# Output projection of a hybrid decoder layer: column groups 2 and 3 as seven products of quarters

## The chip, the core and the metric

The kernel runs on one core of a Trainium2 chip. Its time is the device time of one execution in microseconds (us). An execution is one launch; nothing is computed on the host but a rearrangement of the weights.

## What is computed

One layer on 512 tokens of width 2048, in float32. Two token mixers (latent attention with 16 heads, and a gated spatial unit) give `merged`; then come one output projection, a gate from the conditioning vector, a residual and a final norm. The change touches the last three lines:

```python
c_act = jax.nn.silu(c)                               # c: one row of 2048
mod = c_act @ w_ada + b_ada                          # w_ada: 2048 x 6144
shift, scale, gate = jnp.split(mod, 3, axis=-1)
...
merged = jax.nn.sigmoid(g_mla) * y_mla + jax.nn.sigmoid(g_sgu) * y_sgu   # 512 x 2048
x = x + gate[:, None] * (merged @ w_out)             # w_out: 2048 x 2048
return rmsnorm(x, final_norm_g)
```

## The kernel before, in words

**Products.** TensorE multiplies float32r operands. Each operand is held as a high part (rounded, `hi`) and a low part (the rest, `lo`), and one product takes three matmuls: hi·hi, lo·hi and hi·lo (`mm3`, L156). Weights arrive as raw float32 tiles of 128x1024 (`wraw0` to `wraw2`, 512 KB each). The class `Stream` keeps a list of them in the order of use: it loads up to three ahead on the DMA queue of SP, and splits a tile when it is asked for: ACT rounds it to `w0h` or `w1h` (L121), DVE subtracts to `w0l` or `w1l` (L122).

**The projection.** `merged` stands transposed, one tile of 128 channels x 512 tokens for each of 16 heads: `mh[j]`, `ml[j]` (tile names `b` and `g`). The output has four groups of 512 columns (`cg`) and four blocks of 128 tokens (`n`). `out_granule(cg, i, ...)` (L1784) takes one weight tile, which holds two heads of one column group, and issues 2 x 4 x 3 = 24 matmuls of 128x512 into four PSUM banks: 16 with the high weights (L1795, L1796), then 8 with the low ones (L1793). Eight granules make a group. Granules (0,0) to (0,4) lie beside the last heads of the attention. The last stage, which the change rewrites, has the granules (0,5) to (0,7), groups 1 and 2, and then group 3 in another order: token block by token block, all 16 heads with `mm3`, so that a block ends when its 48 matmuls have run; the last block is done in two halves of 256 columns.

**What stands beside it.** The gate of columns 1024 to 2047 isn't ready yet: eight chunks `wada` of 128x2048 are loaded, multiplied by `cact` and summed on DVE (`chunk_sum`, L1943). `gbc` holds the gate, `gfb` the final gain, both broadcast to all partitions; `yt` holds x and then y for the whole output. `residual` (L1986) takes a finished bank: DVE multiplies by the gate and adds x, ACT squares with a sum (`ssy`), POOL multiplies by the gain. When a token block is complete, `ry` becomes 1/rms (DVE reduce and scale, ACT square root at L2028, DVE reciprocal at L2029), DVE and ACT scale y, and SP issues four DMAs of 256 KB to `out`.

**What sets the order.** Every engine and every DMA queue runs its instructions in the order in which the program writes them; a wait of one holds back all behind it. Nothing reorders them.

**Names that come with the change.** The seven-product scheme cuts an output of 2x2 quarters and an inner dimension of two halves; it needs 7 products instead of 8, and sums of quarters as operands. The kernel uses it earlier already, for the input projections, with a list `V7` of 28 passes (7 products x 4 weight tiles).

Of the kernel before, what the change touches and what calls it, by code (L numbers as in the profile page):

```python
# [20 lines left out]
P = 128  # L21
# [116 lines left out]
def trunk_layer(ctx, tc, xT, xn, c, vecs, pos, wada, w1, w2, wv, wv3, wv4, wh, wh15, wq, wqr, wk, wvv, wo, wsT, bsp, gfin, out,  # L138
# [102 lines left out]
    p_d = [scratch(f"p_d{i}", [10, P, P]) for i in range(2)]  # L241
    latn_d = [scratch(f"latn_d{i}", [P, S]) for i in range(10)]
# [76 lines left out]
    dp = [None]  # L319
    dlast = []  # L320

    def last_tiles():
        k = len(dlast)
        p = last_of[k // 4].p
        dlast.append((nt(p, [P, GW], F32R, f"dh{k}"), nt(p, [P, GW], F32R, f"dl{k}")))
        return dlast[-1]

    last_of = [None, None]
    for cg in range(3):
        for i in range(cg == 0, 8):  # L330
            go[cg, i] = ws.add(wo[cg, i], GW)
            if cg == 2 and i < 6:
                go[3, i] = ws.add(wo[3, i], GW, to=last_tiles)
    for i in (6, 7):
        go[3, i] = ws.add(wo[3, i], GW)
# [1415 lines left out]
    def merge_a(h, ps, turned_, gate_):  # L1751
# [173 lines left out]
    dp[0] = Scope("out", side=RIGHT)  # L1925
    grow = nt(dp[0].p, [P, D], F32, "gbc")
    gfb = nt(dp[0].p, [P, D], F32, "gfb")
    yt = nt(dp[0].p, [P, NB, D], F32, "y")
    last_of[0] = Scope("last", side=RIGHT)
    da = Scope("ada2")  # L1930
    cact = nt(da.p, [P, D], F32, "cact")
    DMA.dma_start(cact, bcast(cact_d, D))
    chunks, later = {}, {}

    def grow_load(cg):
        cols = slice(cg * S, (cg + 1) * S)
        DMA.dma_start(grow[:, cols], bass.AP(tensor=gate_row.tensor, offset=gate_row.offset + cg * S, ap=[[0, P], [1, S]]))

    def chunk_load(j):
        chunks[j] = nt(da.p, [P, D], F32, "wada", bufs=2)  # L1940
        DMA.dma_start(chunks[j], wada[2 * KC + j])

    def chunk_sum(j):  # L1943
        t = chunks.pop(j)
        stt(t, t, 1.0, cact, ALU.mult, ALU.mult, accum_out=dots[:, 2 * KC + j:2 * KC + j + 1])
        if j % 4 == 3:
            gate_sum(j - 3, j + 1)


    for j in range(NG, NG + 2):  # L1950
        chunk_load(j)
    chunk_at = dict(zip(range(NG, KC), (4, 5, 7, 8, 10, 11, 13, 14)))
    for j, st in chunk_at.items():
        later.setdefault(st, []).append(lambda j=j: chunk_sum(j))
        if j + 2 < KC:
            later[st].append(lambda j=j: chunk_load(j + 2))
    rows = []
    for cg, k in ((2, 1), (3, 4)):
        st = chunk_at[4 * cg + 3] + 1
        later.setdefault(st, []).append(lambda cg=cg, k=k: rows.append(  # L1960
            gate_turn(4 * cg, 4 * cg + 4, bank_at(k), nt(tp, [P, S], F32, "sig", bufs=3))))
        later.setdefault(st + 1, []).append(lambda: rows.pop()())
        later.setdefault(st + 2, []).append(lambda cg=cg: grow_load(cg))

    def no_more_chunks():
        da.close()
        last_of[1] = Scope("last1", side=RIGHT)

    later[chunk_at[KC - 1]].append(no_more_chunks)
    def gain_part(q):  # L1970
        cols = slice(q * S, (q + 1) * S)
        DMA.dma_start(gfb[:, cols], bass.AP(tensor=gfin.tensor, offset=gfin.offset + q * S, ap=[[0, P], [1, S]]))

    for cg in range(NG // 4):
        grow_load(cg)
# [33 lines left out]
    while pend:  # L2009
        pend.pop(0)()  # L2010
# [102 lines left out]
```

## Time and profile before

| what | value |
|---|---|
| median of 3 runs | 1530.39 us (1530.23 to 1530.84) |
| the profiled execution, its own time | 1528.86 us |
| its span in the profile | 1527.1 us |
| granted TensorE clock | 0.999 of full speed |
| matmuls | 7104 |
| last stage, first matmul to last | 1370.69 to 1519.62 us of the span |

The span runs from the first instruction to the last; launch and finish are the 1.8 us beside it. In a row of the timeline the first number is the start in us from the span's start, the second the duration, and what stands in brackets is the idle time ahead of it with what ended it. SPq is SP's DMA queue: its rows are the issues of transfers. A TensorE row's duration is longer than its distance from the next, since matmuls are pipelined; the distance is what counts.

### The profile page before, as it was taken

The page shows a single profiled execution, that of the slowest core. Times are in us where ns is not written, and L with a number is a line of the kernel's source. Part 1 is how long each engine was busy: PE and PEld are TensorE (multiplying, and loading weights), DVE is VectorE, ACT ScalarE, POOL GpSimd, SP SyncE. Part 2 cuts the span into 40 slices and gives each one's busy share as a digit, 9 for nine tenths or more (in the row PEclk, how much of TensorE's full clock was granted, in tenths as well). Part 3 has the DMA queues.
Part 4 walks back from the last instruction along what each step waited for, and adds up shares of the span by engine and source line. Part 5 has one row for each costly group of instructions (what it writes and reads, how often), then busy time and mean ns, then how long its engine had stood idle before and what let it go on. Part 6 is the DMA issues. An engine that isn't in the chain of part 4 may idle for free.

```text
span 1527.1 us, 20628 instructions
## 1 busy us (share of the span) xinstructions
PE 1515.8 (99%) x7104; PEld 1268.9 (83%) x7104; DVE 1219.4 (80%) x1656; ACT 816.2 (53%) x1280; POOL 241.2 (16%) x268
## 2 busy tenths in 40 slices
PE   9999999999999999999999999999999999999998
PEld 7888888888888888888888888888888888888887
DVE  8989897768787889888889797878788989856653
ACT  4444665546555556545555556556776677632331
POOL 0000000101010120311040203030242223321120
PEclk9999999999999999999999999999999999999999
DMA  9979876858887796868686967787788888769723
GB/s 376 388 273 349 246 201 171 236 144 239 249 224 188 203 242 198 227 205 215 199 212 188 226 200 188 230 210 215 191 211 204 212 197 231 180 169 348 247 99 111
DMA packets 336427, 337.68 MB, mean 221 GB/s; under 512 B 105801, under 2 KB 279937, under 8 KB 331201
## 3 DMA queue, kind: packets, MB, share of 16 engines
q1 hardware_dynamic: 310082, 306.46, 64.7%
q0 software_dynamic: 26240, 29.89, 11.5%
q8 instruction: 56, 0.92, 0.2%
q14 instruction: 49, 0.40, 0.1%
HBM read 302.12 MB, written 34.17 MB: 220 GB/s over the span
## 4 chain that ended last, share of the span: by engine, by line
PE 91%; DVE 3%; DMA 2%; SPq 1%; ACT 1%; issue 1%; POOL 1%; DVEq 0%; ACTq 0%
PE ps L1476 18%; PE ps L1477 18%; PE ps L1474 18%; PE ps L468 5%; PE ps L1795 3%; PE ps L1796 3%; PE ps L1793 3%; PE ps L158 2%; PE ps L159 2%; PE ps L157 2%; PE ps L477 2%; PE ps L478 2%; PE ps L480 2%; PE ps L1577 2%; PE ps L1578 2%; PE ps L1580 2%
## 5 line engine op out<-in xcount | busy, mean ns | idle before, releaser
L145 DVE TENSOR_TENSOR X<-X,X 128x1024 fp32r<-128x1024 f32 (+2 forms) x111 | 130.5, 1182 | 28.5 <-ACT X L699 27.1
L699 ACT CAST X<-X 128x1024 fp32r<-128x1024 f32 x70 | 73.7, 1053 | 95.7 <-PE ps L1477 55.7
L699 ACT CAST w0h<-X 128x1024 fp32r<-128x1024 f32 x70 | 73.7, 1052 | 93.2 <-PE ps L1477 50.5
L699 ACT CAST w1h<-X 128x1024 fp32r<-128x1024 f32 x69 | 72.6, 1052 | 76.2 <-PE ps L1477 37.1
L145 DVE TENSOR_TENSOR w0l<-X,w0h 128x1024 fp32r<-128x1024 f32 x70 | 85.5, 1221 | 28.8 <-ACT w0h L699 28.7
L145 DVE TENSOR_TENSOR w1l<-X,w1h 128x1024 fp32r<-128x1024 f32 x69 | 84.2, 1221 | 23.5 <-ACT w1h L699 23.5
L145 DVE TENSOR_TENSOR X<-wraw,X 128x1024 f32<-128x1024 f32 (+1 forms) x65 | 79.4, 1221 | 17.8 <-ACT X L699 16.9
L664 POOL DMA_DIRECT2D X<-in_wh x9 | 11.6, 1292 | 509.9 <-DVE w1l L145 166.6
L1477 PE MATMUL ps<-w1h,hl 128*128 128x512 f32 x236 | 91.8, 389 | 0.0
L1476 PE MATMUL ps<-w1h,hh 128*128 128x512 f32 x236 | 91.8, 389 | 0.0
L1476 PE MATMUL ps<-w0h,hh 128*128 128x512 f32 x236 | 91.8, 389 | 0.0
L1477 PE MATMUL ps<-w0h,hl 128*128 128x512 f32 x236 | 91.8, 389 | 0.0
L121 ACT CAST w0h<-wraw 128x1024 fp32r<-128x1024 f32 (+3 forms) x61 | 52.7, 864 | 71.9 <-PE ps L1796 22.9
L1476 PE MATMUL ps<-X,hh 128*128 128x512 f32 x232 | 90.4, 390 | 0.0
L1477 PE MATMUL ps<-X,hl 128*128 128x512 f32 x232 | 90.3, 389 | 0.0
L148 DVE SCALAR_TENSOR_TENSOR wada<-wada,cact 128x2048 f32<-128x2048 f32 x39 | 88.9, 2281 | 0.4 <-DMA wada<-in_wada 0.4
L122 DVE TENSOR_TENSOR w0l<-wraw,w0h 128x1024 fp32r<-128x1024 f32 (+3 forms) x61 | 61.7, 1012 | 34.4 <-ACT w0h L121 20.7
L121 ACT CAST w1h<-wraw 128x1024 fp32r<-128x1024 f32 (+3 forms) x60 | 52.5, 875 | 55.4 <-issue 13.2
L145 DVE TENSOR_TENSOR wraw<-wraw,X 128x1024 f32<-128x1024 f32 x66 | 80.4, 1218 | 0.9 <-DMA X<-in_wv 0.5
L122 DVE TENSOR_TENSOR w1l<-wraw,w1h 128x1024 fp32r<-128x1024 f32 (+3 forms) x60 | 62.7, 1045 | 20.0 <-ACT w1h L121 10.4
L1736 POOL TENSOR_TENSOR d<-turned,d 128x384 fp32r<-128x384 f32 (+1 forms) x48 | 42.7, 918 | 191.8 <-ACT d L1735 191.8
L1474 PE MATMUL ps<-w0l,hh 128*128 128x512 f32 x236 | 63.1, 389 | 0.0
(469 smaller groups left out, 4463.1 us busy)
## 6 DMA issues: line engine op xcount, KB each, us to landing
X<-in_wh SPq DMA_DIRECT2D x131, 512.0 KB, 5.0
wada<-in_wada SPq DMA_DIRECT2D x39, 1024.0 KB, 8.7
wraw<-in_wo SPq DMA_DIRECT2D x32, 512.0 KB, 4.5
wraw<-in_wh SPq DMA_DIRECT2D x21, 512.0 KB, 6.5
wraw<-in_wh POOLq DMA_DIRECT2D x21, 512.0 KB, 7.1
turned<-p_d SPq DMA_DIRECT2D x64, 160.0 KB, 4.6
X<-in_wv SPq DMA_DIRECT2D x17, 512.0 KB, 4.5
X<-in_wh SPq DMA_DIRECT2D x22, 384.0 KB, 4.9
```

Of the source, the lines that this page charges most:

```text
L121: self.nc.scalar.copy(hi[:, :n], raw[:, :n])
L122: self.nc.vector.tensor_tensor(out=lo[:, :n], in0=raw[:, :n], in1=hi[:, :n].bitcast(F32), op=ALU.subtract)
L145: DVE.tensor_tensor(out=out, in0=in0, in1=in1, op=op)
L148: DVE.scalar_tensor_tensor(out=out, in0=in0, scalar=scalar, in1=in1, op0=op0, op1=op1, **kw)
L468: PE.matmul(ps1[m], a[:, cols[m]], b, start=(j == 0 and a is wH and b is hh[j]), stop=False)
L699: ACT.copy(hi, t)
L1474: PE.matmul(to, xh[:, tk], wL[:, k], start=False, stop=sp, skip_group_check=True)
L1476: PE.matmul(to, xh[:, tk], wH[:, k], start=st, stop=False, skip_group_check=True)
L1477: PE.matmul(to, xl[:, tk], wH[:, k], start=False, stop=False, skip_group_check=True)
L1793: PE.matmul(banks[n], mh[j][:, tk], wL[:, sl], start=False, stop=j == H - 1)
L1795: PE.matmul(banks[n], mh[j][:, tk], wH[:, sl], start=j == 0, stop=False)
L1796: PE.matmul(banks[n], ml[j][:, tk], wH[:, sl], start=False, stop=False)
```

## The change

The granules (0,5) to (1,7) stay (eleven "wide" granules). Groups 2 and 3 become one block of 28 "tall" passes of 12 matmuls of 128x512. Its products are called 1 to 7; the list `E7` gives their order, two products interleaved at first (1 with 6, 2 with 7), then 3, 5 and 4.

The merged heads are stored to memory as they are made (`m_d`, 16 DMAs of 256 KB from SP) and read back in pairs j and j+8 beside the wide granules; DVE and ACT make of each pair the operand tiles `S14` and `S2`, and overwrite the right half of `mh[j]`, `ml[j]`. The weight sums of products 6, 2 and 4 are made by DMAs that accumulate into the tile that they land in (`e_add`, issued by POOL), that of product 3 on DVE (`e_third`). The gate's chunks are halves of 128x1024 now (`C0`, `C1`). Of groups 0 and 1, y goes to memory (`y_d`) and comes back at the end; x is added by an accumulating DMA. All output rows are scaled and stored in the last passes and behind them.

A table of steps, `at_(k, phase, f)`, sets the order: k from -22 to -1 are the half granules, 0 to 27 the passes. Cut to its core:

```diff
-    for cg in range(3):
-        ...
-        for i in range(5 if cg == 0 else 0, 8):
-            out_granule(cg, i, pso, ...)
-    wl = [get(go[3, i], 0) for i in range(8)]
-    for n in range(NB):
-        ...                                   # group 3, block by block, with mm3
+            DMA.dma_start(m_d[h], m)          # in merge_a's finish()
...
+    def pair_load(j):
+        raw_m[j] = t = passing_tile().rearrange("p (c w) -> p c w", c=2)   # X0, X1, X5 in turn
+        for c in range(2):
+            DMA.dma_start(t[:, c], m_d[j + 8 * c])
+    def pair_sums(j):
+        a, b = raw_m[j][:, 0], raw_m[j][:, 1]
+        tt(b[:, right], a[:, right], b[:, right], ALU.subtract)
+        tt(a[:, right], a[:, left], a[:, right], ALU.subtract)
+        tt(a[:, left], b[:, right], a[:, left], ALU.subtract)
+        tt(b[:, left], a[:, left], b[:, left], ALU.add)
+        ACT.copy(s14[:, j, 0], b)
+        ACT.copy(s2[:, j, 0], a[:, left])
+    def pair_lows(j):
+        ...                                   # two subtractions on DVE: 512 and 256 columns
+    def pair_third(j):
+        hilo(mh[j][:, right], ml[j][:, right], raw_m.pop(j)[:, 0][:, right])
+    for j, d in enumerate((1, 2, 3, 5, 6, 7, 8, 9)):
+        at_(wide_step(d), SPLIT, pair_sums, j)
+        at_(wide_step(d) + 1, BACK, pair_lows, j)
+        at_(wide_step(max(d, 4 + j // 2)) + 1, BACK, pair_third, j)
+        at_(wide_step((0, 0, 0, 4, 4, 5, 6, 7)[j]) + 1, LOAD, pair_load, j)
...
+    def half_dot(n):                          # on DVE; then loads the chunk after next
+        ...
+        half_load(n + 2)
+    for n, k in enumerate([wide_step(d) for d in (0, 0, 1, 2, 4, 4, 10, 10)] + [2, 4, 5, 6, 8, 9, 10, 11]):
+        at_(k, BACK, half_dot, n)
+    def first_out(g, n, ps):
+        ytile[g, n] = y = nt(xo.p, [P, S], F32, f"Y{n}")
+        tt(y, ps, rows_[g][:, 0], ALU.mult)
+        nc.gpsimd.dma_start(y, xn[n][:, cols_of(g)], accum_op=ALU.add)
+    def first_end(g, n):
+        square_y(n, g, y)                     # ACT
+        nc.gpsimd.tensor_tensor(out=y, in0=y, in1=rows_[g][:, 1], op=ALU.mult)
+        DMA.dma_start(y_d[g][n], y)
...
+    for i in range(4):                        # weights of the passes
+        at_((-11, -6, -4, -2)[i], LOAD, e_kept, i)
+        at_((-9, -5, -3, -1)[i], LOAD, e_add, i, 0, 0)
+        at_((-5, -3, -1, 0)[i], LOAD, e_pass, "11", i)
+        at_(2 * i, LOAD, e_add, i, 1, 4)
+        at_((1, 3, 5, 8)[i], LOAD, e_pass, "22", i)
+        at_((10, 12, 14, 15)[i], LOAD, e_pass, "11b", i)
+        at_((13, 14, 16, 17)[i], EVAC, e_third, i)
+        at_((15, 16, 17, 19)[i], LOAD, e_pass, "21", i)
+        at_((14, 15, 17, 18)[i], LOAD, e_add, i, 0, 4)
+    for g in range(TALL):
+        at_(g - 2, ..., e_split, g)           # ACT rounds; then e_low on DVE
...
+    def c_first(t):                           # t = 0, 1: token blocks 0 and 1
+        o = home["p1"][:, t]
+        tt(o, acc7["w"][t], o, ALU.add)
+        by_row(o, 2)
+        tt(o, o, home["S14"][:, t], ALU.add)
+        square_y(t, CA, o)
+    for t in range(2):
+        at_(24 + t, BACK, c_first, t)
+        at_(26, BACK, r_before, t)            # reduce, scale (DVE)
+        at_(26, BACK, r_of, t)                # square root (ACT), reciprocal (DVE)
+        at_(26 + t, BACK, lambda t=t: row_out(t, ...))   # two scalings on ACT, two on DVE, four DMAs
+        at_(27, BACK, r_before, 2 + t)
...
+    for n in (2, 3):                          # behind the last pass
+        o = home["S2"][:, n]
+        tt(o, acc7["y"][n - 2], home["S2"][:, 6], ALU.mult)
+        tt(o, o, home["S14"][:, n], ALU.add)
+        if n == 3:
+            row_out(2, home["S2"][:, 2], home["z6"][:, 0])
+        square_y(n, CA, o)
+        r_of(n)
+    row_out(3, home["S2"][:, 3], home["z6"][:, 1])
```

**Place 1: SP's queue and ACT at the head of the last stage.** SP's queue before (`cact`, `wada`: the gate's chunks; `gbc`, `gfb`, `y`: gate, gain and x):

```order
L755 DMA gate_row<-sig_12269 8x128
L1932 DMA cact_12308<-cact_d 128x2048
L1941 DMA wada_12310<-in_wada 128x2048
L1941 DMA wada_12312<-in_wada 128x2048
L1937 DMA gbc_12299<-gate_row 128x512 x2
L1972 DMA gfb_12300<-in_gfin 128x512
L1982 DMA y_12301<-in_xn 128x512 x2
L102 DMA wraw_105_12325<-in_wo 128x1024
```

SP's queue now; `X_1794` is the tile of the first pair:

```order
L743 DMA gate_row<-sig_12302 8x128
L1748 DMA m_d_144<-sig_12319 128x512
L1977 DMA CA_12338<-cact_d 128x1024
L1983 DMA C_1785_12340<-in_wada 128x1024
L1983 DMA C_1786_12342<-in_wada 128x1024
L2013 DMA R_1787_12344<-gate_row 128x512
L2013 DMA R_1787_12344<-in_gfin 128x512
L102 DMA wraw_105_12355<-in_wo 128x1024
L1983 DMA C_1792_12382<-in_wada 128x1024
L1983 DMA C_1793_12385<-in_wada 128x1024
L1946 DMA X_1794_12387<-m_d_129 128x512
L1946 DMA X_1794_12387<-m_d_137 128x512
```

ACT there before (`w0h`, `w1h` are the rounded weights of the granules to come; the row at L1993 squares a y):

```order
L121 CAST w1h_12319<-wraw_102_12148 128x1024
L121 CAST w0h_12351<-wraw_103_12200 128x1024
L121 CAST w1h_12382<-wraw_104_12230 128x1024
L121 CAST w0h_12421<-wraw_105_12325 128x1024
L1993 ACTIVATE sig_12432,ssy_12317<-y_12301 128x512
```

ACT now:

```order
L121 CAST w1h_12351<-wraw_102_12180 128x1024
L121 CAST w0h_12396<-wraw_103_12233 128x1024
L1954 CAST S_1783_12337<-X_1794_12387 128x512
L1955 CAST S_1782_12336<-X_1794_12387 128x256
L121 CAST w1h_12437<-wraw_104_12263 128x1024
L1954 CAST S_1783_12337<-X_1795_12390 128x512
L1955 CAST S_1782_12336<-X_1795_12390 128x256
L121 CAST w0h_12481<-wraw_105_12355 128x1024
```

The store of the last head and two more chunk halves stand ahead of the first pair on SP, and the rounding of a pair's sums stands ahead of the rounding of a granule's weights on ACT.

**Place 2: the queues in the first half of the tall block.** SP now, from the third weight tile of the block on (names `wraw`, `X`: weights; `C`, `CA`: chunks). Before there was nothing of the kind; granules of group 2 had one `wraw` each there:

```order
L2051 DMA wraw_1820_12802<-in_wo 128x1024
L2051 DMA X_1821_12808<-in_wo 128x1024
L1983 DMA C_1824_12840<-in_wada 128x1024
L1977 DMA CA_12843<-cact_d 128x1024
L1983 DMA C_1826_12845<-in_wada 128x1024
L2051 DMA wraw_1827_12847<-in_wo 128x1024
L2051 DMA X_1830_12853<-in_wo 128x1024
L2051 DMA X_1836_12878<-in_wo 128x1024
L2051 DMA X_1842_12901<-in_wo 128x1024
L1983 DMA C_1845_12908<-in_wada 128x1024
L2051 DMA X_1850_12945<-in_wo 128x1024
L1983 DMA C_1853_12952<-in_wada 128x1024
```

POOL now, at the same time; all its DMAs here accumulate:

```order
L2051 DMA wraw_1820_12802<-in_wo 128x1024
L2051 DMA wraw_1827_12847<-in_wo 128x1024
L2039 DMA Y_1833_12860<-in_xn 128x512
L2051 DMA X_1808_12619<-in_wo 128x1024
L2039 DMA Y_1839_12884<-in_xn 128x512
L2039 DMA Y_1846_12910<-in_xn 128x512
L2051 DMA wraw_1815_12755<-in_wo 128x1024
L2039 DMA Y_1849_12930<-in_xn 128x512
L2051 DMA wraw_1820_12802<-in_wo 128x1024
L2047 TENSOR_TENSOR Y_1833_12860<-Y_1833_12860,R_1799_12476 128x512
L2051 DMA wraw_1827_12847<-in_wo 128x1024
```

POOL before had only its multiplications by the gain here. From the first row shown up to the load ahead of the last chunk's product there are 18 loads of 512 KB and four stores of 256 KB on SP, and six accumulating loads of 512 KB and four of 256 KB on POOL.

**Place 3: ACT and DVE at the end.** ACT before, the last two blocks (L2028 is the square root, L2033 and L2038 scale y):

```order
L1993 ACTIVATE sig_13248,ssy_12317<-y_12301 128x512
L2028 ACTIVATE ry_12318<-ssy_12317,ry_12318 128x1
L2033 ACTIVATE y_12301<-y_12301,ry_12318 128x512
L1993 ACTIVATE sig_13312,ssy_12317<-y_12301 128x256
L1993 ACTIVATE sig_13369,ssy_12317<-y_12301 128x256
```

ACT now, from the rounding of the last pass's weights (`w0h_13398`) on; L2042 squares, L2149 is the square root, L2155 scales:

```order
L2042 ACTIVATE sig_13382,ssy_12333<-R_1864_13015 128x512
L2080 CAST w0h_13398<-wraw_1827_12847 128x1024
L2042 ACTIVATE sig_13402,ssy_12333<-S_1891_13184 128x512
L2042 ACTIVATE sig_13404,ssy_12333<-S_1891_13184 128x512
L2042 ACTIVATE sig_13409,ssy_12333<-R_1864_13015 128x512
L2042 ACTIVATE sig_13423,ssy_12333<-Z_1868_13038 128x512
L2042 ACTIVATE sig_13425,ssy_12333<-Z_1868_13038 128x512
L2149 ACT_TABLE_LOAD
L2149 ACTIVATE ry_12334<-ssy_12333,ry_12334 128x1
L2155 ACTIVATE S_1902_13251<-S_1902_13251,ry_12334 128x512 x2
L2149 ACTIVATE ry_12334<-ssy_12333,ry_12334 128x1
L2155 ACTIVATE S_1902_13251<-S_1902_13251,ry_12334 128x512 x2
```

DVE now, from the low part of the last pass's weights on:

```order
L145 TENSOR_TENSOR w0l_13399<-wraw_1827_12847,w0h_13398 128x1024
L145 TENSOR_TENSOR R_1864_13015<-ps_1911_13296,R_1864_13015 128x512
L145 TENSOR_TENSOR R_1864_13015<-R_1864_13015,S_1891_13184 128x512
L145 TENSOR_TENSOR R_1864_13015<-R_1864_13015,S_1902_13251 128x512
L2144 TENSOR_REDUCE ry_12334<-ssy_12333 128x1
L154 TENSOR_SCALAR ry_12334<-ry_12334 128x1
L2150 RECIPROCAL ry_12334<-ry_12334 128x1
L148 SCALAR_TENSOR_TENSOR R_1864_13015<-R_1864_13015,ry_12334,S_1891_13184 128x512
L148 SCALAR_TENSOR_TENSOR S_1891_13184<-S_1891_13184,ry_12334 128x512
```

Before, three of four token blocks were finished ahead of the last one; now the norms and the scaling of all four stand behind the last pass's weights in both engines' orders.

More of the change, by code (lines that the diff above doesn't have):

```diff
@@ L318, in trunk_layer @@
                 gr[1] = ws.add(wqr[1], 768)
[L319 to L328, printed above, removed]
[L329 to L335 removed]
+    for cg in range(2):
+        for i in range(cg == 0, 8):
+            go[cg, i] = ws.add(wo[cg, i], GW, to=third_place if (cg, i) == (1, 7) else None)
     pend = []
@@ L1922, in trunk_layer @@
     latp.close()
[L1925 to L1956, printed above, removed]
```

292 lines of the change are left out of this document (216 added, 76 removed).

## Prediction

> **What bounds the kernel now.** I read the page's head and its chain of waits first, then the chain's rows in the last stage, then the timeline of its end.
>
> ```profile
> span 1527.1 us, 20628 instructions
> PE 1515.8 (99%) x7104; PEld 1268.9 (83%) x7104; DVE 1219.4 (80%) x1656; ACT 816.2 (53%) x1280; POOL 241.2 (16%) x268
> PE 91%; DVE 3%; DMA 2%; SPq 1%; ACT 1%; issue 1%; POOL 1%; DVEq 0%; ACTq 0%
> 1467.34 1.81 PE ps L1793 x8
> 1472.78 1.81 PE ps L1793 x8
> 1519.34 0.28 PE L159 MATMUL ps<-w0h,g 128*128 128x256 f32 x1
> 1519.65 0.42 DVE L145 TENSOR_TENSOR sig<-ps,gbc 128x256 f32<-128x256 f32 x1 [3.94 <-PE ps L159]
> 1523.57 0.39 SPq L2040 DMA_DIRECT2D out<-y  x1
> ```
>
> TensorE is busy for 99% of the span and carries 91% of the chain. In the last stage it never stops: two granules are 1472.78 - 1467.34 = 5.44 us apart, .2267 for each of 24 matmuls. Behind its last matmul, which ends at 1519.62, stand DVE, ACT and the last store: 1527.1 - 1519.62 = 7.5 us. So fewer matmuls are worth their whole time if (1) the other engines still keep TensorE fed and (2) what stands behind the last matmul gets no longer. The run profiled took 1528.86, 1.8 more than its span and 1.5 less than the median of 1530.39; I add both to a span.
>
> **1. Matmuls: -12.4.** Group 2 had 8 granules (43.5 us); group 3 ran from 1472.78 + 1.81 = 1474.6 to 1519.6 (45.0). In their place come 28 x 12 matmuls at .2267: 76.2. 88.5 - 76.2 = 12.4 (bounds 12 and 12.5: a pass has the shapes of a granule). With no wait the last matmul would end at 1507.2.
>
> **2. What stands behind the last matmul: +11.1 (8 to 12.5).** Before, three of four token blocks were out; now all norms come last.
>
> ```profile
> 1487.91 0.19 ACT L1993 ACTIVATION_READ_ACCUMULATOR sig<-y 128x1 f32 x1
> 1488.11 1.28 ACT L2028 ACT_TABLE_LOAD   x1
> 1489.41 0.29 ACT L2028 ACTIVATE ry<-ssy,ry 128x1 f32<-128x1 f32 x1
> 1509.60 0.63 ACT L1993 ACTIVATE sig<-y 128x512 f32<-128x512 f32 x1 [9.11 <-DVE y L145]
> 1510.36 0.29 ACT L2028 ACTIVATE ry<-ssy,ry 128x1 f32<-128x1 f32 x1
> 1510.68 0.17 DVE L2029 RECIPROCAL ry<-ry 128x1 f32<-128x1 f32 x1 [1.12 <-ACT ry L2028]
> 1510.94 0.72 ACT L2033 ACTIVATE y<-y,ry 128x512 f32<-128x512 f32 x1 [0.29 <-DVE ry L2029]
> L145 DVE TENSOR_TENSOR sig<-ps,gbc 128x512 f32<-128x512 f32 x15 | 10.3, 683 | 15.4 <-PE ps L159 15.4
> L148 DVE SCALAR_TENSOR_TENSOR y<-y,ry,gfb 128x512 f32<-128x512 f32 x3 | 2.2, 747 | 0.0
> L145 DVE TENSOR_TENSOR w0l<-X,w0h 128x1024 fp32r<-128x1024 f32 x70 | 85.5, 1221 | 28.8 <-ACT w0h L699 28.7
> L121 ACT CAST w1h<-wraw 128x1024 fp32r<-128x1024 f32 x28 | 29.5, 1052 | 32.6 <-issue 13.2 <-PE ps L1796 8.5 <-DMA wraw<-in_w 5.6
> ```
>
> Prices: a square with its sum .75, a DVE product or sum about .7, from square root to reciprocal's end .58, a rounding 1.05, a low part 1.22. Let T be the last matmul's end; a pass is 2.72 us and weights are split two passes ahead, so the rounding for pass 26 starts at T-10.9 and its low part ends at T-8.6. Row block 0 (three DVE operations) ends at -6.4, its square at -5.7. The rounding for pass 27 stands behind that square on ACT: to -4.6; low part to -3.35, in time for pass 27 at -2.7. Then block 1 on DVE to -1.2, its square to -.4, two more squares to +1.05. The table load for the square root (1.28; the row at 1488.11 is the last one before, and it now stands here) ends at +2.35, block 0's square root and reciprocal at +2.9. ACT's two scalings (.72) end at +4.4, block 1's go to +6.5, DVE's last scaling for them to +6.9. Only then, in DVE's order, come blocks 2 and 3, whose banks have long been full: block 2's product and sum to +8.4, square, root and reciprocal to +9.8; block 3's to +11.3 (DVE first scales block 2), square +12.2, reciprocal +12.9, scalings +14.3, last store issued at +15. From the last issue to the span's end it was 1527.1 - 1523.57 = 3.5. Thus T+18.5 against T+7.45. Upper bound: .1 more at each of 14 hand-overs; lower: block 0's square 3 us earlier, so that all behind it moves up.
>
> The Trainium skill ("ScalarE: Activation LUTs", "What ACT_TABLE_LOAD costs") puts a switch of tables at about 1.28 us of load and as much again for a drain, 2.66 together; by that, the tail would be 1.4 us longer, 12.5 in place of 11.1. The trace agrees with the load (1.28) but has the square root at 1489.41, .02 behind its end, and the load .01 behind the instruction ahead: I go by the trace.
>
> **3. Wide granules: +8.0 (2 to 12).** These eleven now have beside them the operand sums: per pair four DVE operations of 256 columns, three more for low parts, casts on ACT.
>
> ```profile
> L145 DVE TENSOR_TENSOR hl<-d,hh 128x256 fp32r<-128x256 f32 x6 | 2.3, 420 | 0.1
> L121 ACT CAST w1h<-wraw 128x512 fp32r<-128x512 f32 x10 | 6.2, 621 | 0.0
> L162 ACT CAST hh<-d 128x256 fp32r<-128x256 f32 x6 | 2.2, 410 | 0.0
> L148 DVE SCALAR_TENSOR_TENSOR wada<-wada,cact 128x2048 f32<-128x2048 f32 x39 | 88.9, 2281 | 0.4 <-DMA wada<-in_wada 0.4
> 1371.61 0.69 DVE L145 TENSOR_TENSOR sig<-sig,b 128x512 f32<-128x512 f32 x1
> 1369.81 0.34 SPq L1932 DMA_DIRECT2D cact<-cact_d  x1
> 1380.00:1390.00 10.00, 10.00 (x45) 8.29 (x45) 5.95 (x7) 2.10 (x2) 0.00 (x0) 1.00 1.00 385
> wraw<-in_wo SPq DMA_DIRECT2D x32, 512.0 KB, 4.5
> ```
>
> Pair 0 is late. On SP the last head's store now stands ahead of the chunks, and it waits until DVE has made that head (1371.61 + .69 = 1372.3), where `cact` was issued at 1369.81 before. Everything behind shifts: the first two chunk products end at about 1377.6 and 1378.9 (half of 2281 each), each lets SP issue a chunk half, and pair 0's two halves follow at 1380.6 to 1381.4. Two 512 KB halves go ahead at the 385 GB/s of 1380 to 1390 (1.36 each), with 4.5 to landing at rest: pair 0 is there at about 1385. Four sums of .46 end at 1386.9, ACT's two casts (.62, .41) at 1387.9, and the rounding for the fourth granule, behind them on ACT, at 1389.0. TensorE wants it at 1370.7 + 3 x 5.44 = 1387.0: 2.0 us of stall. (That 1370.7 is where the first granule's matmuls follow the attention's last heads.) DVE then has per granule 1.22 + 1.84 + 1.16 + 1.2 (a chunk's half) or .7 (an output) = 5.0 to 5.7 of 5.44, so little is caught up. Pair 3 needs the tile X0 back, which pair 0's third sum frees only at 1405.8, behind two chunk products: its weights come 3.2 late at the eighth granule; by the same walk .9 at the sixth, 1.5 at the ninth, .2 and .2 at the last two. Sum 8.0. Low end 2: the first stall alone. High end 12: every DVE operation beside POOL as in the next rows.
>
> ```profile
> 1398.22 1.22 DVE L122 TENSOR_TENSOR w0l<-wraw,w0h 128x1024 fp32r<-128x1024 f32 x1 [3.77 <-PE ps L1793]
> 1403.66 1.55 DVE L122 TENSOR_TENSOR w1l<-wraw,w1h 128x1024 fp32r<-128x1024 f32 x1 [0.68 <-issue]
> 1401.61 2.52 POOL L1995 TENSOR_TENSOR y<-y,gfb 128x512 f32<-128x512 f32 x1 [8.24 <-ACT sig L1993]
> 1478.08 6.33 POOL L1995 TENSOR_TENSOR y<-y,gfb 128x512 f32<-128x512 f32 x4 [13.21 <-ACT sig L1993]
> ```
>
> POOL takes 1.58 for a multiply by itself (6.33 for four) and 2.52 beside DVE; DVE's subtraction beside it takes 1.55 instead of 1.22, .33 more. POOL has the same multiplies for groups 0 and 1 after as before, so they stand in the high end only. The Trainium skill ("SBUF — State Buffer", "SBUF: two separate sides") says that a DVE operation with two SBUF inputs and a GpSimd operation that reads SBUF exclude each other for the whole instruction. By that, four multiplies of 1.58 would hold DVE for 6.3 us; these rows show .33 each, so I keep to them.
>
> **4. Tall passes 0 to 13: +4.5 (0 to 14).**
>
> ```profile
> q1 hardware_dynamic: 310082, 306.46, 64.7%
> q0 software_dynamic: 26240, 29.89, 11.5%
> 602.83 1.28 POOL L664 DMA_DIRECT2D X<-in_wh  x1 [55.36 <-DVE w1l L145]
> 604.80:607.90 3.10, 3.10 (x16) 2.55 (x15) 1.17 (x2) 3.09 (x5) 0.00 (x0) 1.00 1.09 161
> ```
>
> The kernel's input projections use accumulating loads from POOL too. The one issued at 602.83 (512 KB) kept all DMA engines busy at 161 GB/s (the window's last two columns: share, GB/s), and POOL's queue as a whole moved 29.89 MB in 11.5% of 1527 us, 170 GB/s. So 512 KB take about 3.1 us there, 1.36 on SP's queue by the window of term 3. Up to pass 14 the program has 18 loads (24.5), four stores of 256 KB (2.7), six accumulating loads of 512 KB (18.6) and four of 256 KB (6.2): 52 us of transfer against 14 x 2.72 = 38.1 of matmuls. Some of it can be started before the block, and tiles loaded early cover the first passes. Walking the queues, pass 1 is .5 late, pass 4 3.0 (its third `11` weight stands behind two chunk halves, `CA` and a kept tile on SP), pass 14 1.0. Ends: all covered, 0; nothing covered, 52 - 38 = 14. The walk is nearer the low end, since two thirds of the bytes have 5 us or more of slack.
>
> **5. Passes 16 to 18: +2 (0 to 4).** On ACT the rounding for pass 17 waits for a sum of DVE's (`e_third`), and two copies of a bank (.58 each in the row below) stand behind it, which pass 18's product needs: about .8 late. A weight's load stands on SP behind a store that waits for the gate: 1.2.
>
> ```profile
> L915 ACT COPY d<-ps 128x512 f32<-128x512 f32 x80 | 42.5, 583 | 0.0
> ```
>
> The 16 stores of heads in the attention stand in SP's queue behind work that DVE has done by then; loads there have slack of several us. I cost them at 0; without that cover each would add its .3 issue, 5 us.
>
> **Sum.** -12.4 + 11.1 + 8.0 + 4.5 + 2.0 = +13.2: a span of 1540.3, a run of 1542.1, a median of 1543.6.
>
> **Rivals.** *(a) The feeding is hidden* (no change): terms 3 to 5 come to 2 or less, since loads land sooner than I walk; -12.4 + 11.1 + 2 gives 1531. For it: DVE idles some 40% between 1380 and 1390 (5.95 of 10). Against: SP's order, which lets nothing pass the store. *(b) Faster:* the same, and block 0's square root and table load come ahead of T. The place is ACT's queue from T-10.9; it decides if ACT reaches the square root before about T-2, which needs the squares of block 1 to wait for nothing. Then blocks 0 and 1 are out by T+3 and 2 and 3 behind them by T+8: tail +4 at most; -12.4 + 4 + 2 gives 1524. Against: block 1's sums stand behind the low part of pass 27 on DVE, -1.2 at the earliest, unless TensorE itself is late. *(c) The block is bound by transfers:* term 4 at its high end, 14, and all else as in the sum: 1553. For it: 52 against 38 us; against: the start made in the granules ahead.
>
> **How the numbers follow.** My sum .62, (a) .15, (b) .09, (c) .14. A measurement here tells no change from one within 0.2%, 3 us. The sum and (c) are slower (.76), (a) the same (.15), (b) faster (.09). The sum's own range is 1536 to 1550; the range given reaches from (a), 1530, to (c), 1554, and leaves out (b) and a tenth of (c) and (a).
>
> **What would show it.** Step 1: 7104 - 192 - 240 + 336 = 7008 matmuls (group 2, group 3, the block), passes 2.72 us apart. Step 2: the one table load for the square root behind the last matmul, and 18 us from there to the end. Step 3: TensorE idle 2 us ahead of the fourth granule, with ACT's rounding behind `S14` as the releaser; DVE over 95% busy from 1385 to 1430. Step 4: idle time of TensorE ahead of passes 1 and 4 put down to a load; transfers at full share there. Step 5: idle time ahead of passes 16 to 18. I would be wrong above all if pair 0 lands by 1382, if accumulating loads go at the speed of plain ones, or if DVE reaches block 2 ahead of the square roots.

## The result, and the profile after

| | before | after |
|---|---|---|
| median of 6 runs | 1530.62 us (1529.29 to 1531.39) | 1571.55 us (1569.09 to 1573.58) |
| ratio, 95% interval | | 1.0268 [1.0255, 1.0281] |
| span of the profiled execution | 1527.1 us | 1569.8 us |

The change makes the kernel slower by 41 us. The direction was forecast, the size (13 us) was not. The head and the chain's shares of the page after:

```profile
span 1569.8 us, 20726 instructions
PE 1516.8 (97%) x7007; PEld 1263.6 (80%) x7007; DVE 1259.7 (80%) x1731; ACT 841.4 (54%) x1323; POOL 252.8 (16%) x287
PE 76%; DVE 8%; DMA 7%; issue 3%; ACT 3%; SPq 2%; POOL 0%; DVEq 0%; ACTq 0%
```

There are 97 matmuls fewer, but TensorE's share of the chain fell from 91% to 76%; DVE and transfers took ten of these fifteen points. TensorE's waits in the last stage (waiting line, releaser: us in total, times, longest), where there were none before:

```profile
PE ps L1784 <- ACT w1h L121: 12.8, 2, 6.7
PE ps L2205 <- ACT w1h L2080: 8.3, 2, 6.2
PE ps L2205 <- ACT Z L2106: 4.3, 1, 4.3
PE ps L2001 <- DVE gate L145: 2.6, 1, 2.6
PE ps L2205 <- ACT w0h L2080: 1.1, 1, 1.1
PE ps L1784 <- ACT X L121: 0.5, 1, 0.5
```

That is 29.6 us of idle time. ACT is named as the releaser, but ACT waited itself. The chain shows for what: pieces of it, in order of time, at the stalls ahead of the fourth and the eighth granule and through the tall block (`C`: chunk halves; `X<-m_d`: pairs; `X<-in_wo`: weights):

```profile
1376.25 6.80 DMA C<-in_wada
1383.14 1.23 DVE C L148 x2
...
1386.72 6.40 DMA X<-m_d
...
1395.98 0.95 ACT w1h L121
1396.98 0.80 PE ps L1784
...
1412.46 9.99 DMA X<-m_d
...
1458.67 10.62 DMA X<-in_wo
...
1477.48 9.66 DMA C<-in_wada
...
1488.49 8.88 DMA C<-in_wada
...
1498.73 5.87 DMA C<-in_wada
...
1515.16 8.51 DMA X<-in_wo
```

Each long piece is a transfer of 512 KB or, for a pair, of 256 KB, from issue to landing: 6 to 11 us, where 512 KB of weights took 4.5 in the median before. The transfers of the last stage as a whole, in windows (the last two columns are the busy share of the DMA engines and GB/s); first two of before (granules; token blocks), then three of after (wide granules; passes 0 to 18; the rest):

```profile
1371.00:1474.00 103.00, 103.00 (x457) 85.05 (x456) 62.67 (x64) 32.83 (x43) 13.94 (x8) 1.00 0.76 270
1474.00:1520.00 46.00, 45.62 (x243) 38.86 (x241) 18.61 (x38) 9.92 (x23) 7.07 (x5) 1.00 0.19 69
```

```profile
1374.00:1453.00 79.00, 64.60 (x265) 51.79 (x263) 51.38 (x86) 23.70 (x45) 11.97 (x10) 0.91 0.80 239
1453.00:1527.00 74.00, 58.79 (x233) 46.71 (x234) 44.38 (x51) 25.58 (x34) 18.88 (x18) 0.91 0.95 272
1527.00:1552.00 25.00, 25.00 (x105) 20.46 (x104) 18.76 (x25) 10.87 (x19) 3.48 (x4) 0.93 0.86 236
```

GB/s times us gives the bytes: 28 + 3 = 31 MB before, 19 + 20 + 6 = 45 MB after. In the tall block the DMA engines are busy 95% of the time while TensorE is busy for 59 of 74 us. For that window the two queues (packets, MB, share):

```profile
q1 hardware_dynamic: 4521, 14.32, 52.2%
q0 software_dynamic: 1870, 5.76, 42.6%
```

14.32 MB in .522 x 74 us are 371 GB/s, 1.41 us for 512 KB; POOL's accumulating loads get 5.76 MB in .426 x 74, 183 GB/s, 2.9 us. The queues together took 70 us for what stands beside 19 passes, 52 us of matmuls.

The end, from the last matmul on, with rows of TensorE, ACT, DVE (block 2's sums, block 3's sums) and SP:

```profile
1551.91 0.61 PE L2207 MATMUL ps<-w0l,b 128*128 128x512 f32 x2
1552.22 1.28 ACT L2149 ACT_TABLE_LOAD   x1
1553.52 0.29 ACT L2149 ACTIVATE ry<-ssy,ry 128x1 f32<-128x1 f32 x1
1558.03 0.68 DVE L145 TENSOR_TENSOR S<-ps,S 128x512 f32<-128x512 f32 x1
1560.63 0.67 DVE L145 TENSOR_TENSOR S<-ps,S 128x512 f32<-128x512 f32 x1
1565.90 0.58 SPq L2158 DMA_DIRECT2D out<-Z  x1
```

From 1552.5 to 1569.8 are 17.3 us, 9.8 more than before. The last store is issued 13.4 behind the last matmul.

### The profile page after: what moved, and what is told of

The parts are those of the page before. It is cut to its first block, busy times and chain, and to the rows that moved or that the text cites. A ratio compares the mean times of both kernels' runs of the same rounds, so it can differ in the third digit from the quotient of the medians.

```text
span 1569.8 us, 20726 instructions
## 1 busy us (share of the span) xinstructions
PE 1516.8 (97%) x7007; PEld 1263.6 (80%) x7007; DVE 1259.7 (80%) x1731; ACT 841.4 (54%) x1323; POOL 252.8 (16%) x287
## 3 DMA queue, kind: packets, MB, share of 16 engines
q0 software_dynamic: 29696, 39.33, 14.6%
## 4 chain that ended last, share of the span: by engine, by line
PE 76%; DVE 8%; DMA 7%; issue 3%; ACT 3%; SPq 2%; POOL 0%; DVEq 0%; ACTq 0%
PE ps L1464 18%; PE ps L1465 18%; PE ps L1462 18%; PE ps L456 5%; PE ps L466 2%; PE ps L465 2%; PE ps L468 2%; DMA C<-in_wada 2%; SPq L1708 2%; DMA X<-in_wo 1%; DVE X L145 1%; DMA turned<-p_d 1%; PE ps L1565 1%; DMA X<-m_d 1%; PE ps L1566 1%
## 5 line engine op out<-in xcount | busy, mean ns | idle before, releaser
L145 DVE TENSOR_TENSOR X<-X,X 128x1024 fp32r<-128x1024 f32 (+2 forms) x118 | 140.9, 1201 | 29.6 <-ACT X L687 26.8
L145 DVE TENSOR_TENSOR w1l<-X,w1h 128x1024 fp32r<-128x1024 f32 x75 | 91.6, 1221 | 37.3 <-ACT w1h L687 24.2
L145 DVE TENSOR_TENSOR w0l<-X,w0h 128x1024 fp32r<-128x1024 f32 x77 | 94.0, 1221 | 29.4 <-ACT w0h L687 27.6
L687 ACT CAST w1h<-X 128x1024 fp32r<-128x1024 f32 x69 | 72.6, 1052 | 77.7 <-PE ps L1465 37.3
L145 DVE TENSOR_TENSOR X<-wraw,X 128x1024 f32<-128x1024 f32 (+1 forms) x71 | 86.7, 1221 | 22.8 <-ACT X L687 17.0
L148 DVE SCALAR_TENSOR_TENSOR wada<-wada,cact 128x2048 f32<-128x2048 f32 x31 | 70.7, 2282 | 0.4 <-DMA wada<-in_wada 0.4
L121 ACT CAST w1h<-wraw 128x1024 fp32r<-128x1024 f32 (+3 forms) x55 | 47.2, 858 | 43.9 <-issue 13.2
L121 ACT CAST w0h<-wraw 128x768 fp32r<-128x768 f32 (+3 forms) x55 | 46.4, 844 | 44.6 <-issue 12.7
L122 DVE TENSOR_TENSOR w0l<-wraw,w0h 128x768 fp32r<-128x768 f32 (+3 forms) x55 | 54.1, 984 | 15.0 <-ACT w0h L121 10.7
L122 DVE TENSOR_TENSOR w1l<-wraw,w1h 128x1024 fp32r<-128x1024 f32 (+3 forms) x55 | 55.5, 1010 | 9.8 <-ACT w1h L121 9.0
```

What stands on the lines that cost most here:

```text
L121: self.nc.scalar.copy(hi[:, :n], raw[:, :n])
L122: self.nc.vector.tensor_tensor(out=lo[:, :n], in0=raw[:, :n], in1=hi[:, :n].bitcast(F32), op=ALU.subtract)
L145: DVE.tensor_tensor(out=out, in0=in0, in1=in1, op=op)
L148: DVE.scalar_tensor_tensor(out=out, in0=in0, scalar=scalar, in1=in1, op0=op0, op1=op1, **kw)
L687: ACT.copy(hi, t)
```

## Experiments

**How they are compared.** One run each, beside a run of the kernel before (1528.7 to 1531.0). The stage's first matmul starts anywhere from 1369.6 to 1374.0 in kernels whose attention is the same, so I compare lengths from there: wide granules (59.8 without a wait: 11 x 5.44), tall block (76.2), end (last matmul to the span's end) and stage (first matmul to the span's end), worked out from the timeline rows of TensorE and good to .1. The two rows from which before and after are reckoned:

```profile
1370.69 0.45 PE L1795 MATMUL ps<-w0h,b 128*128 128x512 f32 x1
```

```profile
1373.70 0.45 PE L1784 MATMUL ps<-w0h,b 128*128 128x512 f32 x1
```

| kernel | run, us | wide | tall | end | stage |
|---|---|---|---|---|---|
| before | 1530.6 | | | 7.5 | 156.4 |
| after | 1571.6 | 79.3 | 99.5 | 17.3 | 196.1 |
| pairs_first | 1568.8 | 77.6 | 100.2 | 17.2 | 195.1 |
| no_dots | 1563.6 | 75.8 | 94.5 | 17.5 | 187.9 |
| no_chunks | 1540.7 | 65.7 | 84.2 | 18.1 | 167.9 |
| plain_adds | 1562.5 | 78.7 | 92.6 | 18.0 | 189.3 |
| pool_pairs | 1564.0 | 73.9 | 97.9 | 18.0 | 189.8 |
| tail_early | 1569.9 | 80.2 | 100.8 | 14.7 | 195.7 |
| pool_tail | 1564.4 | 73.6 | 103.9 | 13.3 | 190.7 |
| fill | 1572.0 | 77.8 | 101.4 | 18.0 | 197.2 |
| light | 1541.5 | 69.7 | 77.7 | 18.2 | 165.5 |
| gain_dve_free | 1540.8 | 63.6 | 85.2 | 18.1 | 167.0 |
| gain_dve | 1567.0 | 77.6 | 100.1 | 18.0 | 195.7 |
| gate_before | 1610.4 | 64.9 | 82.8 | 18.2 | 165.9 |
| gate_before_end | 1602.5 | 63.0 | 81.3 | 14.5 | 158.8 |
| all_three | 1612.4 | 69.8 | 82.4 | 14.6 | 166.8 |
| gate_spread | 1577.8 | 63.4 | 84.0 | 14.5 | 161.9 |

**Order or transfers.** Theory A: the stalls come from the written order of SP and DVE. Theory B: the stage has more to transfer than its time allows.

`pairs_first`, the same transfers in another order:

```diff
+    for j in range(3):
+        pair_load(j)
     silu_load(0)
     half_load(0)
```

> The loads of pairs 0 to 2 stand at the head of SP's queue, ahead of the gate's first chunk halves. Theory A, order: the stall ahead of the fourth granule (6.7 us idle and 2.0 of slow clock behind it) comes from the pair's place in the queue; pair 0 lands some 6 us sooner, the stall falls below 1 us, and the run takes 1560 to 1566 instead of 1571.5. Theory B, transfers: the same bytes have to pass, the chunks come later by as much, their products hold DVE, and the run stays within 3 us of 1571.5.

The stall ahead of the fourth granule did go (.5 left), but one of 2.9 came in the third, where DVE was now late, and the one at the eighth granule grew from 6.1 to 8.0. The stage is 1.0 shorter, as theory B says.

`no_dots` and `no_chunks`, a pair: the first leaves out the products of the late chunk halves, the second their loads as well.

```diff
-        stt(t, t, 1.0, ca[0], ALU.mult, ALU.mult, accum_out=dch[...])     # both
-        DMA.dma_start(t, wada[2 * KC + j][:, half_cols[e]])               # no_chunks
-        DMA.dma_start(ca[0], ...)                                         # no_chunks
```

> The 16 products of the gate's late chunk halves are left out on DVE, the loads stay (the late half of the gate is a constant). Bytes are as before, but neither DVE nor SP waits for a chunk's product any more. Theory A, order (waits for chunks hold DVE and SP, and what stands behind them comes late): the idle times of 6.7, 4.3 and 2.6 us go, with their slow clock, 1550 to 1556. Theory B, transfers: the stalls of the block stay or move, at most 7 us are won, 1564 to 1571.

> Products and loads of the gate's late chunk halves are left out (16 loads of 512 KB and two of the activated row; the late half of the gate is a constant). Theory A: about as the kernel that leaves out the products alone, within 4 us of it. Theory B: 9 MB less at 1.36 us for 512 KB are 24 us of transfer, of which the stalls give back what they hold: at least 10 us faster than the kernel without the products alone, about 1543 to 1553.

Without the products the stage is 8.2 shorter, a little better than B's share and far from A's. Without the bytes it is 20.0 shorter again: 18 transfers, 1.1 us each, against 1.4 for 512 KB alone. This pair answers the question: of the 39.7 us by which the stage is longer than before, the products of the chunks with the waits for them are a fifth, the bytes of the same chunks half.

`plain_adds`:

```diff
-        e_fill(nc.gpsimd, ekept[i], g, o + i, accum_op=ALU.add)
+        e_fill(nc.gpsimd, ekept[i], g, o + i)
```

> The 12 accumulating loads of weights become plain ones from the same queue into the same tiles (the weight sums are wrong). Theory A: what waits is order, not rate; under 4 us faster, 1567 to 1572. Theory B: twelve times 3.1 - 1.36 us are 21 us less of transfer, all in the tall block; the stalls ahead of its third and sixth passes shrink and the run takes 1555 to 1563.

The stage is 6.8 shorter, the tall block 7.0: B's range, but a third of the 21 us that its prices would give. Part of it is that the loads didn't get the price of SP's queue: POOL's queue, with four loads of 256 KB that still accumulate, moved 295 GB/s here (6.22 MB in 30.1% of the 70 us from 1450 to 1520), not 371. That the other transfers hold the rest is not shown.

`pool_pairs`, the pairs without transfers:

```diff
-            DMA.dma_start(m_d[h], m)
-            DMA.dma_start(t[:, c], m_d[j + 8 * c])
+            nc.gpsimd.tensor_tensor(out=t[:, c], in0=mh[h], in1=ml[h], op=ALU.add)   # h = j + 8 * c
```

> No stores of heads and no loads of pairs: POOL adds the high and the low part of a head into the pair's tile instead (two additions of 128x512 for a pair). Theory B, transfers bound the last stage: 16 stores and 16 loads of 256 KB at .7 are 22 us of transfer less, half of it beside the wide granules; the two stalls there (6.7 and 6.1 us idle, 4 of slow clock) shrink below 3 together, the stage starts up to 1.7 sooner, and the run takes 1555 to 1560. Theory C, DVE's chain of sums is what is late: the stalls stay, 1567 to 1572.

The stage is 6.3 shorter, between B and C: the stall ahead of the fourth granule is gone, but 2.05 stand ahead of the eighth, 1.0 inside it and 5.2 ahead of the ninth. The start of the stage (1372.4) lies among those with the stores.

`light` takes all of it together: no late chunks, plain loads, pairs on POOL.

> Three edits at once: no late chunks of the gate (a constant instead), the 12 accumulating loads plain (the weight sums are wrong), pairs made on POOL. If transfers are what keeps TensorE waiting, next to nothing of the waits is left: under 4 us of idle time and 2 of slow clock in the last stage, its matmuls end within 6 us of 136.3 (11 granules and 28 passes without a wait) after its first, and the run takes 1530 to 1536, the longer end being what is left of the loss. If DVE's pair sums or ACT's order bound it too, 7 us or more of idle stay and the run takes 1538 or more.

The tall block now runs in 77.7, 1.5 above its matmuls alone: with these transfers gone, the 23 us that its stalls cost are gone. TensorE's waits in the stage:

```profile
PE ps L1783 <- ACT w0h L121: 4.7, 1, 4.7
PE ps L2204 <- ACT w0h L2079: 1.1, 2, 0.9
PE ps L1783 <- ACT w1h L121: 0.9, 1, 0.9
PE ps L1783 <- ACT X L121: 0.6, 1, 0.6
```

But the wide granules keep 7.2 us of idle time, with the slow clock behind it 10 us; here my expectation was wrong, and the rival (DVE's sums) right. The longest wait, 4.7, stands ahead of the ninth granule, and ACT's rounding for it stands behind a pair's sums on DVE. DVE beside POOL's additions in that trace, a subtraction of low parts first, then the four sums ahead of that wait:

```profile
1401.51 3.79 DVE L122 TENSOR_TENSOR w0l<-wraw,w0h 128x1024 fp32r<-128x1024 f32 x1 [2.84 <-ACT w0h L121]
1398.90 5.31 POOL L1947 TENSOR_TENSOR X<-b,g 128x512 f32<-128x512 f32 x4
1415.62 4.54 DVE L145 TENSOR_TENSOR X<-X 128x256 f32<-128x256 f32 x4
1416.60 2.80 POOL L1947 TENSOR_TENSOR X<-b,g 128x512 f32<-128x512 f32 x2
```

The subtraction that takes 1.22 took 3.79; POOL's block of additions runs from 1398.90 to 1404.21, and 1404.21 + 1.22 is 1405.4, near the 1405.3 at which DVE is done. The four sums, 1.8 by themselves, took 4.54. So this wait comes in with the pairs on POOL, an edit of this run (`pool_pairs` has it too), and is none of the changed kernel's own.

**Does POOL shut DVE out?** (theory E) `gain_dve_free` (on `no_chunks`) and `gain_dve` (on the changed kernel) move the product with the gain:

```diff
-        nc.gpsimd.tensor_tensor(out=y, in0=y, in1=rows_[g][:, 1], op=ALU.mult)
+        tt(y, y, rows_[g][:, 1], ALU.mult)
```

> On the kernel without the late chunks (a constant half of the gate): the products of y with the gain move from POOL to DVE, .69 each. There, from the seventh granule on, a granule takes up to 6.3 us instead of 5.44, and the four sums of a pair take 2.3 to 3.5 beside POOL's product instead of 1.8. Theory E, POOL's product shuts DVE out while it runs: the sums go back to 1.8 in each granule, the chain of a granule loses .5 to 1.7 and gains .7 only where it is in its way, the stalls of the wide granules fall from 4.4 to below 2.5, 1537 to 1539. Rival, the sums wait for something else: DVE has .7 more for each granule, the stalls grow to 6 to 8, 1542 to 1545.

> The same move in the changed kernel itself. Theory B: the block behind is set by transfers, so what DVE wins beside the wide granules is waited for again later; within 2.5 us of 1571.5. If DVE's chain there carried the loss, 3 us or more faster.

The four sums of a pair in the changed kernel, beside POOL's product, and in `gain_dve_free`:

```profile
1440.51 1.71 POOL L2047 TENSOR_TENSOR Y<-Y,R 128x512 f32<-128x512 f32 x1 [4.59 <-ACT sig L2042]
1440.99 2.89 DVE L145 TENSOR_TENSOR X<-X 128x256 f32<-128x256 f32 x4
```

```profile
1425.83 1.79 DVE L145 TENSOR_TENSOR X<-X 128x256 f32<-128x256 f32 x4
```

The first two of those four sums of the changed kernel in the chain:

```profile
1440.99 1.52 DVE X L145
1442.54 0.44 DVE X L145
```

The first, .44 by itself, took 1.52 and ended at 1442.5, within .2 of the end of POOL's product (1442.2) plus its own time; with POOL quiet all pairs take 1.79 or 1.80. So E's mechanism holds: the later wide granules lost part of their waits (wide 65.7 to 63.6). Its time does not: `gain_dve_free` took 1540.8 instead of 1537 to 1539, and the stages are only 1.0 and .4 shorter. `gain_dve`'s run is 4.6 below the changed kernel's, which by the number alone is its rival; but its stage began 4.1 sooner, which this edit does not touch. Part of what was won ahead of the block was waited for in it (84.2 to 85.2; 99.5 to 100.1).

**The slow clock.** Behind a long stall matmuls stood .43 apart instead of .23, here until 1400.8, 3.8 us long:

```profile
1396.98 0.80 PE L1784 MATMUL ps<-w1h,b 128*128 128x512 f32 x1 [6.71 <-ACT w1h L121]
1397.57 0.63 PE L1785 MATMUL ps<-w1h,g 128*128 128x512 f32 x1
1398.00 0.63 PE L1784 MATMUL ps<-w1h,b 128*128 128x512 f32 x1
```

It came five times; the granule or pass behind each of these stalls took 1.7 to 2.6 longer than its 5.44 or 2.72, 11 us in sum. `fill` puts matmuls that nobody reads into two stalls:

```diff
     for d in range(WIDE):
+        for _ in range({3: 24, 7: 24}.get(d, 0)):
+            PE.matmul((pso1 if d == 3 else pso)[0], mh[8][:, 0:P], mh[9], start=True, stop=True)
```

> 24 matmuls of 128x512 whose result nothing reads stand ahead of the fourth and of the eighth wide granule (5.4 us each), in what was idle time of 6.7 and 6.1. Theory D, the slow clock behind a stall comes from the idle time ahead of it: with 1.3 and .7 us of idle left, the clock stays full, the granules behind take 2.0 and 2.1 less, and the run is 3 to 4 us faster, 1567 to 1568.5. Rival: the slow clock has another cause, the run stays at 1571.5 within 1.5.

The clock did what theory D said. The window from 1380 to 1400, in after and in `fill` (the clock is the last column but two):

```profile
1380.00:1400.00 20.00, 13.29 (x53) 10.61 (x52) 10.19 (x19) 1.89 (x4) 0.00 (x0) 0.85 0.86 293
```

```profile
1380.00:1400.00 20.00, 19.47 (x86) 15.82 (x85) 11.53 (x21) 3.23 (x6) 0.00 (x0) 1.00 0.86 295
```

The time did not follow: the DMA share is the same, the wide granules became 1.5 shorter, the tall block 1.8 longer, and the stage took 197.2. So in these two stalls the slow clock cost next to nothing of its own: what was won was waited for again further on.

**The end.** `tail_early` and `pool_tail` finish blocks 0 and 1 in passes 24 to 26, and block 2 ahead of block 3:

```diff
-        at_(24 + t, BACK, c_first, t)
-        at_(26, BACK, r_of, t)
-        at_(26 + t, BACK, row_out ...)
+        at_(24, BACK, c_first, t)
+        at_(25, BACK, r_of, t)
+        at_(26, BACK, row_out ...)
```

> Order alone, at the end: rows of blocks 0 and 1 are finished (sums, norm, scaling, store) in passes 24 to 26 instead of 24 to 27 and behind; block 2 is finished ahead of block 3. Theory of the prediction's term 2 (the end is a chain of ACT and DVE in their written order): from the last matmul to the span's end 9 to 10.5 us instead of 17.4, the run 1563 to 1566. Rival: DVE and ACT are late for the last weights then, TensorE ends later by as much, 1570 to 1573.

> Both edits together: pairs made on POOL, and the end in the earlier order. If the two act apart, their gains add up: 1547 to 1553, still slower than before, with the stalls of the tall block left (13 to 15 us of idle, 7 of slow clock). If the end only hides what the block loses, 1555 to 1560.

The end fell to 14.7 and 13.3, not to 10, and the block grew by 1.3 (`tail_early` beside the changed kernel) and 6.0 (`pool_tail` beside `pool_pairs`): the last weights' rounding now stood behind the squares of both blocks on ACT, and TensorE waited 1.1 and 2.9 for it. For `tail_early` the rival is right; `pool_tail`, with 1564.4, is above both of its ranges.

**Is there room elsewhere?** `gate_before` sums the whole gate beside the attention (32 more pieces of 128x512, six in a row in every second head); `gate_before_end` adds a new end (squares of blocks 0 and 1 behind the last rounding), `all_three` also the pairs on POOL.

```diff
-NG = 8
-PIECES = (0, 1, 0, 2, 2, 1) + (2,) * 9 + (0,)
+NG = 16
+PIECES = (0, 1, 0, 7) + (2, 6) * 6
-    half_load(0)                              # and all that stands for late chunks
```

> All of the gate's columns are summed beside the attention, in pieces of 128x512 (32 more of 256 KB there), none in the last stage: nothing of the result is left out. Theory B, transfers of the last stage: it comes near the kernel without chunks, 1540.7, plus what the attention takes for 32 more sums of .75 on DVE and 8 MB, 0 to 8 us: 1541 to 1549. Theory A, order of DVE and SP: the products alone gave 8 us, so 1558 to 1564. If the attention is bound by its transfers too, they cost there what they save here: 1560 to 1570.

> As the kernel with the whole gate ahead, and the end in another order: squares of blocks 0 and 1 behind the last weights' rounding, their roots and scalings in passes 25 and 26, block 2's sums ahead of the scalings. With TensorE no longer waiting for transfers near the end, the time from the last matmul to the end falls from about 18 to 10 to 11 us and TensorE ends no later: 7 us faster than the run with the gate ahead alone. If DVE and ACT make the last weights late again, under 3 us faster.

> The gate ahead, the new end, and pairs made on POOL instead of stored and loaded. If transfers are what is left of the stalls (some 9 us of idle, 4 of slow clock without chunks), 8 MB less bring 5 to 8 us more: 1526 to 1533, on a level with the kernel before. If DVE's chain of sums is what is left, within 2 us of the run with the gate ahead and the new end.

The stage became as short as without chunks, 165.9, and 158.8 with the new end: `gate_before_end` is 7.9 faster than `gate_before`, as expected, though its end of 14.5 misses the 10 to 11. But the stage began at 1442 instead of 1373, so that `gate_before` and `all_three` lie far above what was expected of them. DVE stood waiting for one piece after the other. Two of the waits between 1000 and 1440 in `gate_before`:

```profile
PE ps L1661 <- DVE hl L145: 51.8, 6, 12.0
DVE piece L148 <- DMA piece<-in_wada: 46.2, 19, 4.3
```

`all_three` shows POOL's additions again as a burden: the wide part takes 69.8 instead of 63.0.

`gate_spread` issues one piece at a time at four or five places of a head, with the new end, the gain on DVE, and two evacuations ahead of a rounding:

```diff
+        peaks()
+        if h > 2:
+            step()                            # one piece; likewise at the other places
-    at_(7, EVAC, lambda: h_copy("p1", ...))
+    at_(7, START, lambda: h_copy("p1", ...))
```

> Nothing of the result is left out. The whole gate ahead of the last stage, but one piece at a time at four or five places of a head instead of six in a row; the end as in the run with the gate ahead and the new end; the gain on DVE; the two copies of a finished bank ahead of the next rounding on ACT. Last stage (first matmul of its first granule to the span's end) was 158.8 us with gate and end alone, 156.4 in the kernel before; evened stalls take 3 to 4 off: 154 to 157. If the attention's loss of 70 us came from bursts in which DVE waits for one piece after the other, it falls below 15 and the run takes 1528 to 1545; if it came from the bytes and sums themselves, it stays above 40 and the run takes 1570 or more.

Spreading the pieces took 29 of the 70 us away; the stage begins at 1414.1, still 40 late, and the run is slower than the changed kernel. What of these 40 is bytes and what order I have not told apart. The stage, 161.9, missed its 154 to 157. In none of the runs is the stage shorter than the 156.4 of before.

## Why the prediction was wrong

Terms 1 and 2 came out: -12.9 and +9.8 against -12.4 and +11.1. Terms 3 to 5, TensorE's waits, were forecast at 14.5 in sum and measured 42.8; this makes the miss. That the direction came out was not luck: the longer end and the stalls at the fourth and eighth granule and at pass 4 stand where they were forecast. But the three signs of being wrong that the prediction named all pointed to a shorter time, and none of them came.

- **Term 1, matmuls (-12.4): right.** 7007 matmuls (7008 forecast). Without waits the wide granules and the block take 59.8 + 76.2 = 136.0; from first to last matmul it was 148.9 before: -12.9. `light` comes to 147.4; the 11.4 above are nearly all waits and slow clock.
- **Term 2, the end (+11.1; 8 to 12.5): right**, +9.8. The table load stood at the last matmul's end (T), and blocks 2 and 3 came behind the scalings of 0 and 1, as walked. ACT reached the first root at T+1.0 instead of T+2.35, and the last store was issued at T+13.4 instead of T+15. The drain of about 1.4 us that the Trainium skill adds to a table load ("ScalarE: Activation LUTs", "What ACT_TABLE_LOAD costs") is not in the rows: the root starts at 1553.52, .02 behind the load's end.
- **Term 3, wide granules (+8.0; 2 to 12): mis-sized**, 79.3 - 59.8 = +19.5. The places were right (fourth and eighth granule), the sizes 6.7 and 6.1 of idle instead of 2.0 and 3.2, with 4.2 of slow clock behind them. The step that failed: pair 0 "is there at about 1385", with 3.7 us for the first chunks and 4.5 at most for the pair; they took 6.8 and 6.4, pair 3 10.0. Pair 0 landed at 1393.1, 8 us later, 3 of them because the stage began later. I took a landing time at rest for a queue in which chunks, gate and gain rows, weights and three pairs were put at once. DVE was not full: it was busy for 27 of the 45 us from 1385 to 1430, 61% where I expected over 95%.
- **Terms 4 and 5, tall block (+4.5 and +2.0): mis-sized**, 99.5 - 76.2 = +23.3, beyond the upper ends of both (18). Prices per transfer were good (3.1 forecast, 2.9 measured; 1.36 and 1.41), and the count of 52 us against 38 pointed the right way. What failed is the sentence that chose between the ends: "the walk is nearer the low end, since two thirds of the bytes have 5 us or more of slack". The DMA engines were busy for 80% of the wide granules and 95% of passes 0 to 18, where 70 us of transfer stood beside 52 of matmuls, so little slack was left. Of the places only pass 4 was right (6.2 of idle instead of 3.0); the others were passes 0, 9, 13 and 19 (1.1, 4.3, 2.6 and 2.1), not 1, 14 and 16 to 18. Rival (c) named the mechanism, with a chance of .14; its 1553 was still 18 short. The right step was to set all bytes of the stage, wide and tall, against the DMA engines' rate.
- **Within term 3, POOL beside DVE: the reading of the row was wrong.** I took .33 for a subtraction that stood beside POOL. In that row (1403.66 of before) DVE was issued when POOL's product had .5 left; the .33 was the rest of an exclusion, not its price. Where DVE's operation comes early in POOL's, the price was more: +1.1 for a sum of .44. The rule of the Trainium skill that I set aside ("SBUF — State Buffer", "SBUF: two separate sides"), that such operations exclude each other for the whole instruction, agrees with these rows. It hardly sets the time here: without it, in `gain_dve`, the stage is .4 shorter.
- **At nothing:** the slow clock behind a stall, 11 us in sum, has no term; `fill` won nothing back by removing it from two stalls. And the head stores. The stage began 3.0 later than in the one profile of before, but over the kernels with the same attention it varies by 4.4, and the three without the stores begin at 1372.0 to 1374.0. A cost of the stores is not seen; whether the change itself costs 1 to 2 us there stays open.

## What to carry to other kernels

Before an edit that saves matmuls, add up all bytes of its stage by queue and price, ahead of and within the block, and set them against the stage's new time; a slack per transfer, read from a trace at rest, is not room when the sum is over. Where transfers set the pace, a gain ahead of them can be lost again at the next landing: here a shorter chain on DVE (`gain_dve`), a full clock (`fill`) and another order (`pairs_first`, `tail_early`) changed the stage by 1.1 us at most, the chunks' products by 8.2, their bytes by 20.0. A row that shows two engines side by side tells the whole price of a contention only where the second one comes early in the first one's operation.

## What the runs showed of the hardware

- DVE operations with two SBUF inputs that met POOL operations on SBUF ended about their own time behind POOL's end: a subtraction of 1.22 us took 3.79, a sum of .44 took 1.52.
- An accumulating load from POOL's queue moved 183 GB/s, plain loads on SP's 371 in the same 74 us. In `plain_adds`, where only four loads of 256 KB still accumulate in the window, POOL's queue moved 295 GB/s.
- After 6.7 us of idle time matmuls ran at about half rate (.43 us apart) for 3.8 us, as the Trainium skill has it ("TensorE: Matmul & The Clock Gate", "What's actually happening") for idle times of about 3.4 us or more. Here 2.1 us of idle at 1526.1 were followed by it as well, and 2.6 at 1507.4 were not, so a shorter idle time can be enough.
